# A streaming encoder's mixer: the third convolution input moved ahead of the query latents' split, the fourth into the attention stage, the output weights tied to the fifth head

## The chip, the cores and the metric

The kernel runs on one core of a Trainium2 chip. The metric is the device time of one execution in microseconds (us), as a median over runs. Engines are named as in the profile: PE is TensorE (matrix products; PEld its weight loads), DVE is VectorE, ACT is ScalarE, POOL is GpSimd, SP is SyncE, which here only issues DMAs. L145 means line 145 of the kernel.

## The reference, cut to what matters

Two layers of a Conformer-like block on 512 tokens of width 1024, all in float32:

```python
for l in range(2):
    x = x + 0.5 * swiglu(rms_norm(x), w_gate, w_up, w_down)      # FFN 1, inner width 2816
    h = rms_norm(x);  p = h @ w_in                               # the mixer's one input projection
    attn = mla_group(p[:384], p[384:640], p[640:672], ...)       # query latent, key/value latent, rotary key
    conv = conv_group(p[672:], ...)                              # GLU, causal depthwise conv k=31, LayerNorm, swish
    x = x + concat([attn, conv]) @ w_out
    x = x + 0.5 * swiglu(rms_norm(x), ...)                       # FFN 2
    x = rms_norm(x)
```

`mla_group` makes 8 heads of queries and keys from the latents (96 wide, RMS-normed, 32 of them rotated), chunk-causal scores, a softmax, and values of width 64. `conv_group` gates 512 channels and convolves each with its own 31 taps.

## The kernel before

**Layout and precision.** Features lie on partitions in tiles of 128, tokens along the free axis (512). Every float32 weight or activation that meets a matmul is split into a high part (an ACT cast to the matmul type, L134 or L150-157) and a low part (the rest, a DVE subtraction, L140 or L152-158), and `mm3` (L144) issues three matmuls for each product: high x high, high x low, low x high. These are the lines L145, L146 and L147.

**Loading.** `load_w` (L129) asks SP for a 128x1024 weight tile in a `raw` buffer (3 of them), lets ACT cast it to `wh` (4 buffers) and DVE subtract it to `wl` (4 buffers). With kind "sum", used for the first four output weight tiles, ACT writes the negated high part instead (L137) and a DMA issued by POOL (L138) adds the weights onto it in memory.

**The mixer of one layer** (`mix_body`, L527). The list `SEQ` (L44) gives the order of the steps after the first convolution input (L696):

- `q0 R c1 q1 q2`: query latents 0 to 2 (`latent_q`), the spread of the row norm R, and the second convolution input c1;
- `qo`: the split of the three query latents (`latent_q_out`, L157/L158, and their squares L174/L177);
- `k kt tt`: the key/value latent, its transposes (L620), the small per-token terms;
- `uq uk`: queries and keys from the latents. For each of four token blocks of keys, ACT copies and squares, DVE reduces, POOL raises to the power -1/2 (`rsqrt`, L163, tile `sck`), and DVE scales the keys into `kn` (L690 and L692). The last of these `rsqrt` instructions is kept as `order["keys"]`;
- `c2 c3`: the third and fourth convolution inputs.

`conv_in(c)` (L542) is two groups of 8 products, so 48 matmuls of 512 columns into two PSUM banks; `glu` (L531) follows: two DVE products with R (L533, L537), a sigmoid on ACT (L535) and a DVE product (L539) that writes u[c]. Convolutions 0 and 3 ("D") run their 30 taps on DVE (L814) into a PSUM bank; 1 and 2 ("A") run them as an ACT product (L818) and a POOL addition (L822) for each tap.

**Attention.** A loop over steps (L797) runs five stages with lags, from `ORDER`: `turn` (transposes of queries and keys of a head on PE, L718 and L723, then ACT L720 and DVE L725), `scores` one step later (L741 and the mask L742; DVE maxima L743; ACT exponentials L747), `turn_p` three later (L762, copies L765), `values` four later (L775, L780, L782) and `turn_out` five later (L793). So `turn(1)` comes before `scores(0)` in the text.

**What sets the order.** The text gives each instruction its rank; a planner then fixes, for each engine, the order in which its queue issues, taking by rank what its own timing says is ready, with buffers of one pool tag handed out from a fixed number. On the chip each engine runs its queue in that order and waits at semaphores. `tc.issue_after(i)` ties the instructions of its block to `i`: those of the block that run on the same engine as `i` are queued behind `i`; those of other engines get no tie. Three such ties matter here: the output weights' block (L803) behind `order["keys"]`, a POOL instruction; the POOL additions of convolution 1 from tap shift 16 on and all of convolution 2 (L821), behind the same one; and the early output groups (L829) behind the last scores.

**After attention.** POOL adds the four convolution outputs (L836 to L838), a matmul with a matrix of 1/512 gives their mean (L840), DVE subtracts it (L846), squares are summed (L178, L183), POOL takes the power, L197/L201 spread it, DVE and ACT finish the LayerNorm and swish (L856, L858), and the output projection runs over the attention part (which needs only `at`) and then the convolution part. Two of its groups come after the mean's matmul in the text, a third after the sums, and a fourth after the spread.

Of the kernel before, what the change touches and what calls it, by code (L numbers as in the profile page):

```python
# [39 lines left out]
WIDE = 5  # L40
CONV = "DAAD"
PAUSE = 16
SEQ = "q0 R c1 q1 q2 qo k kt tt uq uk c2 c3"
POOLW = "wo"  # L44
QFOLD = 0
GLUP = 0
# [24 lines left out]
def encoder_kernel(ctx: ExitStack, tc: tile.TileContext, xT, consts, vecs, rgain, wgu1, wd1,  # L71
# [20 lines left out]
    def tmp(w=S, dt=FP):  # L92
        return tmps.tile([P, w], dt, tag="t", name=nm("t"))

    def bank():
        return psum.tile([P, S], FP, tag="ps", name=nm("ps"))
# [32 lines left out]
    def load_w(src, w, kind="", two=False):  # L129
        raw = wpool.tile([P, WC], FP, tag="raw", name=nm("raw"), bufs=3)  # L130
        to = raw[:, :w]
        nc.sync.dma_start(out=to.rearrange("p (m c) -> p m c", m=2) if two else to, in_=src)
        hi = wpool.tile([P, WC], FR, tag="wh", name=nm("wh"))
        A.copy(hi[:, :w], raw[:, :w])  # L134
        lo = wpool.tile([P, WC], FR, tag="wl", name=nm("wl"))
        if kind == "sum":
            A.activation(lo[:, :w], raw[:, :w], AF.Copy, scale=-1.0)  # L137
            G.dma_start(out=lo[:, :w], in_=src, accum_op=ALU.add)  # L138
            return hi, lo
        (G if kind in POOLW.split() else V).tensor_tensor(lo[:, :w], raw[:, :w], hi[:, :w].bitcast(FP),  # L140
                                                          ALU.subtract)
        return hi, lo
# [67 lines left out]
    def group(o, w, rhs, ks, n):  # L210

        for k in ks:
            c = slice(k * P, (k + 1) * P)
            mm3(o, w[0][:, c], w[1][:, c], rhs[k][0], rhs[k][1], k == 0, k == n - 1)
# [308 lines left out]
    def mix(l, gx, norm, done):  # L523
        with tc.tile_pool(name="k", bufs=4) as kpool:
            mix_body(kpool, l, gx, norm, done)

    def mix_body(kpool, l, gx, norm, done):  # L527
        u, order = [], {}
        ys = [None if kind == "D" else kpool.tile([P, S], FP, tag="y", name=nm("y"), bufs=2) for kind in CONV]

        def glu(pa, pg):  # L531
            tg = tmp()
            V.tensor_tensor(tg, pg, R, ALU.mult)  # L533
            sg = tmp()
            A.activation(sg, tg, AF.Sigmoid)  # L535
            ta = tmp()
            V.tensor_tensor(ta, pa, R, ALU.mult)  # L537
            uc = slot()
            (G if GLUP else V).tensor_tensor(uc, ta, sg, ALU.mult)  # L539
            u.append(uc)  # L540

        def conv_in(c):  # L542
            pp = []
            for j in range(2):
                ps = bank()
                group(ps, load_w(wcv[l, 2 * c + j], WC, f"c{c}"), gx, range(KD), KD)
                pp.append(ps)
            glu(*pp)
# [148 lines left out]
        rm = norm()  # L697
        for step in SEQ.split():
            if step == "R":
                R = norm()  # L700
# [12 lines left out]
        heads = [{} for _ in range(H)]  # L713
# [83 lines left out]
        for step in range(H + 6):  # L797
            for stage, lag in STAGES:
                if 0 <= step - lag < H:
                    stage(step - lag)  # L800


        with tc.issue_after(order["keys"]):  # L803
            wo = [load_w(wout[l, m], WC, "sum") for m in range(WOP)]
        cw, cb = vv(l, "cw"), vv(l, "cb")
        for c in range(4):
# [4 lines left out]
            for k in range(CK - 2, -1, -1):  # L811
                s = CK - 1 - k
# [41 lines left out]
        for c in range(4):  # L854
            z = tmp()
            V.tensor_tensor(z, ys[c], pr, ALU.mult)  # L856
            s = tmp()
# [217 lines left out]
```

## Time and profile before

| | |
|---|---|
| median of 3 runs | 1817.16 us (1814.3 to 1822.64) |
| the profiled execution's own time | 1818.46 us |
| its span, first to last instruction | 1816.7 us, mean granted PE clock 0.993 |
| PE busy | 1761.6 us, 97% of the span |
| DVE, ACT, POOL busy | 1405.7, 949.7, 280.1 us |
| mixer of layer 1, about | 352 to 563 us |
| mixer of layer 2, about | 1250 to 1461 us |

A timeline row gives the start, the duration, the engine, the line, the operation, the tiles and, in brackets, how long the engine sat idle before it and what released it. Matmuls are pipelined: the start-to-start distance, not the shown duration, is what one costs. A row of the view of windows gives, for a stretch, its length and then for each engine its busy time and number of instructions; behind them stand the granted PE clock, the DMA share and GB/s.

### The profile page before, as it was taken

The page shows a single profiled execution, that of the slowest core. Times are in us where ns is not written, and L with a number is a line of the kernel's source. Part 1 is how long each engine was busy: PE and PEld are TensorE (multiplying, and loading weights), DVE is VectorE, ACT ScalarE, POOL GpSimd, SP SyncE. Part 2 cuts the span into 40 slices and gives each one's busy share as a digit, 9 for nine tenths or more (in the row PEclk, how much of TensorE's full clock was granted, in tenths as well). Part 3 has the DMA queues.
Part 4 walks back from the last instruction along what each step waited for, and adds up shares of the span by engine and source line. Part 5 has one row for each costly group of instructions (what it writes and reads, how often), then busy time and mean ns, then how long its engine had stood idle before and what let it go on. Part 6 is the DMA issues. An engine that isn't in the chain of part 4 may idle for free.

```text
span 1816.7 us, 22175 instructions
## 1 busy us (share of the span) xinstructions
PE 1761.6 (97%) x8160; PEld 1448.8 (80%) x8160; DVE 1405.7 (77%) x1983; ACT 949.7 (52%) x1471; POOL 280.1 (15%) x216
## 2 busy tenths in 40 slices
PE   8899999999899999999998999999999999999997
PEld 6688888888688778888876888888978787788885
DVE  8968887588958968878779678866989679678864
ACT  6444445457954634445544444444778445444442
POOL 4000000048932000000000000000688300000000
PEclk9999999999999999999999999999999999999998
DMA  8344434324124345343924445343250543444241
GB/s 287 122 156 152 149 105 139 117 87 127 37 115 117 125 154 163 113 142 107 286 70 131 136 129 162 105 128 118 74 151 1 161 118 119 159 139 153 91 151 58
DMA packets 119037, 234.09 MB, mean 129 GB/s; under 512 B 10256, under 2 KB 55696, under 8 KB 118928
## 3 DMA queue, kind: packets, MB, share of 16 engines
q1 hardware_dynamic: 115040, 219.72, 36.9%
q0 software_dynamic: 3456, 12.58, 3.9%
q8 instruction: 64, 1.05, 0.2%
q14 instruction: 45, 0.37, 0.1%
q10 hardware_dynamic: 432, 0.38, 0.1%
HBM read 207.47 MB, written 25.17 MB: 128 GB/s over the span
## 4 chain that ended last, share of the span: by engine, by line
PE 65%; issue 19%; DVE 5%; DMA 3%; ACT 3%; POOL 1%; SPq 1%; POOLq 0%; DVEq 0%; ACTq 0%
PE ps L145 20%; PE ps L147 20%; PE ps L146 20%; PE ps L775 2%; PE ps L741 1%; DVE wl L230 1%; DMA fr<-in_wgu 1%; ACT pr L818 1%; DMA r<-d 1%; PE ps L762 1%; DMA d<-e 1%; DVE fr L326 1%; ACT r L747 1%; POOL sck L163 0%; PE ps L201 0%
## 5 line engine op out<-in xcount | busy, mean ns | idle before, releaser
L145 PE MATMUL ps<-wh,r 128*128 128x512 f32 (+2 forms) x1392 | 520.3, 386 | 19.0 <-ACT wh L228 8.5
L147 PE MATMUL ps<-wh,r 128*128 128x512 f32 (+2 forms) x1392 | 530.8, 386 | 7.3 <-DVE r L158 7.1
L146 PE MATMUL ps<-wl,r 128*128 128x512 f32 (+2 forms) x1392 | 532.5, 384 | 0.0
L228 ACT CAST wh<-fr 128x1024 fp32r<-128x1024 f32 x256 | 267.9, 1049 | 239.2 <-PE ps L147 143.4
L147 PE MATMUL ps<-r,wl 128*128 128x512 f32 x1008 | 390.8, 390 | 0.5 <-POOL wl L140 0.5
L146 PE MATMUL ps<-r,wh 128*128 128x512 f32 x1008 | 391.1, 390 | 0.0
L145 PE MATMUL ps<-r,wh 128*128 128x512 f32 x1008 | 385.7, 393 | 3.2 <-ACT r L384 1.8
L230 DVE TENSOR_TENSOR wl<-fr,wh 128x1024 fp32r<-128x1024 f32 x256 | 312.6, 1224 | 76.2 <-ACT wh L228 75.2
L145 PEld LDWEIGHTS ps<-wh,r 128*128 128x128 f32 x1392 | 262.0, 189 | 73.8 <-ACT wh L228 10.3
L147 PEld LDWEIGHTS ps<-wh,r 128*128 128x128 f32 x1392 | 262.4, 189 | 62.5 <-DVE r L158 11.8
L146 PEld LDWEIGHTS ps<-wl,r 128*128 128x128 f32 x1392 | 262.4, 188 | 50.6 <-DVE wl L230 0.5
L134 ACT CAST wh<-raw 128x1024 fp32r<-128x1024 f32 (+2 forms) x150 | 148.8, 996 | 239.3 <-PE ps L146 89.2
L145 PEld LDWEIGHTS ps<-r,wh 128*128 128x128 f32 x1008 | 188.7, 188 | 48.3 <-ACT r L384 4.7
L146 PEld LDWEIGHTS ps<-r,wh 128*128 128x128 f32 x1008 | 189.2, 188 | 42.1 <-DVE r L385 1.8
L147 PEld LDWEIGHTS ps<-r,wl 128*128 128x128 f32 x1008 | 189.2, 188 | 40.8 <-POOL wl L140 1.3
L140 DVE TENSOR_TENSOR wl<-raw,wh 128x1024 fp32r<-128x1024 f32 (+3 forms) x134 | 157.6, 1177 | 76.4 <-ACT wh L134 75.6
L163 POOL TENSOR_TENSOR rtok<-vtok,minus_half 128x4 f32<-128x4 f32 x9 | 12.0, 1329 | 1089.4 <-DVE vtok L189 1089.4
L822 POOL TENSOR_TENSOR y<-y,pr 128x509 f32<-128x509 f32 (+15 forms) x120 | 157.8, 1316 | 49.9 <-ACT pr L818 42.4
L326 DVE TENSOR_TENSOR fr<-fr,fr 128x1024 f32<-128x1024 f32 x112 | 136.7, 1222 | 7.4 <-DMA fr<-in_wgu 7.2
L467 DVE TENSOR_TENSOR x<-ps,x 128x512 f32<-128x512 f32 x128 | 86.5, 686 | 44.1 <-PE ps L147 43.7
L385 DVE TENSOR_TENSOR r<-r,r 128x512 fp32r<-128x512 f32 x88 | 58.4, 682 | 70.7 <-ACT r L384 70.5
L356 ACT ACTIVATE e<-e,rtok 128x256 f32<-128x256 f32 x120 | 59.8, 507 | 71.6 <-DVE e L347 70.7
(164 smaller groups left out, 1724.1 us busy)
## 6 DMA issues: line engine op xcount, KB each, us to landing
fr<-in_wgu SPq DMA_DIRECT2D x176, 512.0 KB, 4.0
raw<-in_wd SPq DMA_DIRECT2D x64, 512.0 KB, 4.5
d<-e SPq DMA_DIRECT2D x176, 128.0 KB, 2.7
r<-d SPq DMA_DIRECT2D x88, 256.0 KB, 4.0
raw<-in_wd SPq DMA_DIRECT2D x32, 384.0 KB, 3.8
raw<-in_wcv SPq DMA_DIRECT2D x16, 512.0 KB, 3.3
raw<-in_wout SPq DMA_DIRECT2D x16, 512.0 KB, 3.7
raw<-in_wgu SPq DMA_DIRECT2D x8, 512.0 KB, 4.7
```

Of the source, the lines that this page charges most:

```text
L134: A.copy(hi[:, :w], raw[:, :w])
L140: (G if kind in POOLW.split() else V).tensor_tensor(lo[:, :w], raw[:, :w], hi[:, :w].bitcast(FP), ALU.subtract)
L145: T.matmul(o, lh, rh, start=first, stop=False, skip_group_check=free)
L146: T.matmul(o, lh, rl, start=False, stop=False, skip_group_check=free)
L147: T.matmul(o, ll, rh, start=False, stop=last, skip_group_check=free)
L228: A.copy(hi[:, :w], src[:, :w])
L230: V.tensor_tensor(lo[:, :w], src[:, :w], hi[:, :w].bitcast(FP), ALU.subtract)
L326: V.tensor_tensor(oh, ah, bh, ALU.add)
L356: A.activation(out[j][:, :h], src[j][:, :h], AF.Silu, scale=r)
L385: V.tensor_tensor(d, d.bitcast(FP), hi.bitcast(FP), ALU.subtract)
L467: V.tensor_tensor(xm, pd.rearrange("p (a t j) -> p t a j", a=4, t=NT), xm, ALU.add)
L822: order["conv"] = G.tensor_tensor(acc[:, s:], acc[:, s:], pr[:, s:], ALU.add).ins
```

## The change

The third convolution input moves from the end of the sequence to a place ahead of `qo`. The fourth leaves the sequence and is issued in the attention loop, in the step with number 1, right after the stage `turn`; so in the text it stands behind the transposes of heads 0 and 1 and ahead of `scores(0)`. The block that loads the first four output weight tiles is tied to the last instruction of `scores(4)`, a PE matmul, instead of to the last key `rsqrt`.

```diff
-SEQ = "q0 R c1 q1 q2 qo k kt tt uq uk c2 c3"
+SEQ = "q0 R c1 q1 q2 c2 qo k kt tt uq uk"
...
             for stage, lag in STAGES:
                 if 0 <= step - lag < H:
                     stage(step - lag)
+                if stage is turn and step == 1:
+                    conv_in(3)
...
-        with tc.issue_after(order["keys"]):
+        with tc.issue_after(heads[4]["s"]):
             wo = [load_w(wout[l, m], WC, "sum") for m in range(WOP)]
```

No instruction is added or removed by the text; only ranks and ties change. The POOL additions of the convolutions keep their tie to `order["keys"]`.

## Prediction

> **What bounds the kernel now.** The page first: TensorE is busy almost throughout, so only what moves its idle stretches, or its clock, can move the time.
>
> ```profile
> PE 1761.6 (97%) x8160; PEld 1448.8 (80%) x8160; DVE 1405.7 (77%) x1983; ACT 949.7 (52%) x1471; POOL 280.1 (15%) x216
> ```
>
> Then the view of windows over the first mixer. From its first product to the end of the four convolution inputs PE has no gap; around the start of attention it has one, and the granted clock falls with it.
>
> ```profile
> 352.00:452.00 100.00, 100.00 (x509) 87.02 (x508) 78.76 (x128) 61.98 (x112) 58.69 (x44) 1.00 0.33 98
> 450.00:460.00 10.00, 5.90 (x33) 4.52 (x32) 4.47 (x8) 9.98 (x16) 9.61 (x10) 0.95 0.80 181
> 460.00:470.00 10.00, 9.68 (x51) 6.32 (x50) 9.60 (x19) 9.99 (x24) 9.29 (x8) 0.88 0.20 42
> ```
>
> The timeline of PE shows the gap: the transposes of heads 0 and 1, then 4.10 us until the first scores.
>
> ```profile
> 452.01 0.60 PE L718 MATMUL ps<-cst,q 128*96 128x128 f32 x4
> 452.45 0.60 PE L723 MATMUL ps<-cst,kn 128*96 128x128 f32 x4
> 452.89 0.60 PE L718 MATMUL ps<-cst,q 128*96 128x128 f32 x4
> 453.32 0.60 PE L723 MATMUL ps<-cst,kn 128*96 128x128 f32 x4
> 458.02 0.49 PE L741 MATMUL ps<-r,r 96*128 96x128 f32 x2 [4.10 <-ACT r L720]
> ```
>
> ACT's timeline says why L720 came so late: output weight casts and convolution taps, then the fourth input's sigmoid, stand ahead of it.
>
> ```profile
> 453.12 1.03 ACT L134 CAST wh<-raw 128x1024 fp32r<-128x1024 f32 x1
> 454.05 1.05 ACT L137 ACTIVATE wl<-raw 128x1024 fp32r<-128x1024 f32 x1
> 455.01 0.69 ACT L818 ACTIVATE pr<-r,vec 128x487 f32<-128x487 f32 x1
> 455.60 0.61 ACT L535 ACTIVATE t<-t 128x512 f32<-128x512 f32 x1
> 456.12 1.27 ACT L818 ACTIVATE pr<-r,vec 128x486 f32<-128x486 f32 x2
> 457.30 1.24 ACT L720 ACTIVATE r<-ps,gqs 96x512 f32<-96x512 f32 x2
> ```
>
> What the gap is worth: 4.1 us idle, and in the two windows a clock short by 0.05 and 0.12 of 10 us each, 1.7 us more; 5.8 us a layer, 11.6 in both at most. The change aims there: 48 matmuls between the transposes and the first scores.
>
> [...]
>
> **A second bound, on POOL.** Most additions of convolutions 1 and 2 are queued behind the last key `rsqrt`. From there POOL works without a break until the convolution outputs are added.
>
> ```profile
> 438.75 2.75 POOL L163 TENSOR_TENSOR sck<-ssk,minus_half 128x8 f32<-128x8 f32 x1 [0.99 <-DVE scp L689]
> 441.46 0.92 POOL L138 DMA_DIRECT2D wl<-in_wout  x1
> ...
> 508.04 1.27 POOL L838 TENSOR_TENSOR t<-t,r 128x512 f32<-128x512 f32 x1
> ```
> ```profile
> L822 POOL TENSOR_TENSOR y<-y,pr 128x496 f32<-128x496 f32 (+29 forms) x45 | 57.4, 1276 | 4.2 <-ACT pr L818 1.2
> L138 POOL DMA_DIRECT2D wl<-in_wout x4 | 3.5, 880 | 0.0
> ```
>
> So the run from 441.5 to 509.3 is 67.8 us, of which 45 additions of 1.276 us are 57.4. Its result feeds the mean's matmul:
>
> ```profile
> 515.71 0.65 PE L793 MATMUL ps<-cst,t 128*128 128x128 f32 x4 [0.79 <-DVE t L782]
> 516.20 1.02 PE L840 MATMUL ps<-t,onesm 128*128 128x512 f32 x2
> ```
> ```profile
> 530.15 0.50 PE L145 MATMUL ps<-r,wh 128*128 128x512 f32 x1 [0.17 <-ACT r L151]
> ```
>
> The mean's matmul starts at 516.2 behind the last attention transposes: POOL has 6.9 us to spare. From there to the first product that needs the convolution (530.15) is a chain of 13.95 us, with the early output groups as PE's cover.
>
> **The change, step by step: the third input.** One matmul costs (452.01 - 430.25)/96 = 0.227 us, from the first matmul of the third input to the first transpose behind the fourth.
>
> ```profile
> 430.25 0.39 PE L145 MATMUL ps<-r,wh 128*128 128x512 f32 x1
> ```
>
> So 48 are 10.9 us, and everything from the latents to the keys comes 10.9 us later: the keys' last product at 441.1 instead of 430.25. PE had no gap where the input now goes, so nothing is won there. It brings two casts and two splits (1.03 on ACT, 1.22 on DVE each) and the `glu`; DVE has 21 us free in the 100, which hide them; uncovered they would cost some 5. The query latents' split now stands behind this `glu`. That order binds: in the trace the split starts right behind the sigmoid of the second input, though the first latent's products had ended by 369.66, when the spread follows them on PE.
>
> ```profile
> 369.66 1.02 PE L201 MATMUL ps<-t,ones 128*128 128x512 f32 x2
> ```
> ```profile
> 382.43 0.63 ACT L535 ACTIVATE t<-t 128x512 f32<-128x512 f32 x1
> 382.97 0.67 ACT L157 ACTIVATE r<-ps,vec 128x512 fp32r<-128x512 f32 x1
> ```
>
> I read this as buffers of one tag being handed out in the order of the text. The split's cover is then the key latent's matmuls; I take 0 for it, and up to 2 us if the squares come late.
>
> **The POOL run.** The last `rsqrt` moves with the keys, 10.9 us, less what leaves its path. DVE's rows show two splits of the fourth input's weights in that path; in the changed order they come earlier, in the place that the third's had.
>
> ```profile
> 435.05 1.22 DVE L140 TENSOR_TENSOR wl<-raw,wh 128x1024 fp32r<-128x1024 f32 x1
> 436.19 0.23 DVE L685 TENSOR_SCALAR ssk<-ssk,ckc 128x8 f32<-128x8 f32 x1
> 436.32 0.42 DVE L692 TENSOR_TENSOR kn<-ck,scp 128x256 f32<-128x256 f32 x1
> ...
> 444.24 1.48 DVE L692 TENSOR_TENSOR kn<-ck,scp 128x256 f32<-128x256 f32 x1
> ```
>
> Two times 1.22 is 2.4, so it ends at 441.5 + 10.9 - 2.4 = 450.0, and POOL's run at 517.8: 1.6 us behind today's 516.2. The second layer:
>
> ```profile
> 1333.51 4.22 POOL L163 TENSOR_TENSOR sck<-ssk,minus_half 128x8 f32<-128x8 f32 x2 [1.01 <-DVE ssk L685]
> 1337.68 0.91 POOL L138 DMA_DIRECT2D wl<-in_wout  x1
> ...
> 1404.02 1.26 POOL L838 TENSOR_TENSOR t<-t,r 128x512 f32<-128x512 f32 x1
> ```
> ```profile
> 1413.40 1.02 PE L840 MATMUL ps<-t,onesm 128*128 128x512 f32 x2
> ```
>
> `rsqrt` ends at 1337.7, POOL at 1405.3, the mean starts at 1413.4: 8.1 to spare. Here I take only one split off (its `rsqrt` wait is shorter): 10.9 - 1.2 - 8.1 = 1.6 us late. Bounds of the shift per layer: all of 10.9 (4.0 and 2.8 late), or 6 us, when neither is late.
>
> **The fourth input.** It should fill the 4.1 us. But the keys' last step ends at 445.7, 15.5 us after their last product; today two inputs (21.8 us) lie over that, afterwards one at most. If PSUM banks too are handed out in the order of the text, the input cannot start before the last bank of `turn(1)` is taken, thus before the first block of keys is ready. That is at 436.74, 6.5 us behind the keys' end; less the split at 435.05 it is 5.3. PE would fill 0.9 of it with the query transposes (two times 0.44) and idle 4.4. Then come 48 matmuls and the key transposes, and first scores at 441.1 + 5.3 + 10.9 + 0.9 = 458.2, against 458.02. The gap is moved, not closed; clock loss likewise. If banks go by readiness, the gap is 0 to 4 us; if every key block were needed, see below. In all but the last case attention ends before POOL's 517.8.
>
> **The output weights.** The block holds SP, ACT and POOL instructions and no PE one, so a tie to a PE matmul ties nothing; what goes is POOL's tie. Loads, casts and the POOL issues then come when buffers fall free, which is at the keys' end and during the fourth input, about as late as now. I take 0. It could gain up to 2.4 us a layer (four issues at some 0.6 us leave the POOL run), or cost 2.1 (POOL waits for one L134 and L137 ahead of the last `rsqrt`).
>
> **The sum.** 1.6 + 1.6 = 3.2 us on the profiled 1818.46, thus 1821.7. That execution lies 1.3 above the median of 1817.16, so the median becomes 1820.4; I say 1820.5, +0.2%. Half a per cent is 9.1 us, about what a measurement here can tell from no change (the three runs spread over 8.3 us); the edges are 1808.1 and 1826.2.
>
> **Rivals.** *The gap closes (faster).* The planner starts the fourth input at once, the transposes fall into it, and a less crowded DVE shortens the path from the keys to the last `rsqrt`. Then 5.8 us a layer come back (the second layer taken like the first): 1817.2 - 11.6 = 1805.6. For it: that path is 11.2 us today (441.5 - 430.25), and only part of it is the keys' own work. Against it: for the whole gain POOL must be done by 516.2 - 5.8 = 510.4, so its run must begin by 442.6, only 1.5 us after the keys' last product. Half of it, without passing the bound, is in my forecast. Chance 0.12.
>
> *PE waits for the whole of the keys (slower).* The place is PE's queue: transposes of all four key blocks ahead of the fourth input. PE then stands from 441.1 until the last block, 15.5 - 2.4 = 13.1 us, and first scores come at 441.1 + 13.1 + 10.9 + 0.9 = 466.0, 8.0 late, in both layers: 1817.2 + 16 = 1833. It decides as soon as the last blocks' transposes stand ahead of more than some 5 us of the input. Against it: the transposes depend on the keys block by block. Chance 0.16.
>
> *The tie does hold (slower).* If the weights really come in the fifth head, 4 x 2.1 = 8.4 us of ACT land where ACT is as full as in the quoted window (9.99 of 10). Taps give way and POOL's run stretches; if half is absorbed, 4.2 a layer: 1825.6. Chance 0.05.
>
> **How the numbers follow.** Forecast 0.67, rivals 0.12, 0.16, 0.05. Range 1811 to 1830: it takes in POOL's bounds (0 to 6.8 in sum), the 2 us of the latents' split in both layers, half of the gap won, and most of the slower rival; about 0.1 lies outside on each side. Faster by over half a per cent 0.11 (the first rival nearly whole), slower 0.19 (the second, a part of the third and the forecast's tail), same 0.70.
>
> **What would show it.** In the changed profile: the last `sck` near 450, with L822 running unbroken to about 517; L840 then released by POOL, not by L793; PE's idle time between keys and fourth input instead of ahead of the first scores; output weight casts still near 445 to 458. L840 at or before 516 with no gap ahead of the scores would refute me on the fast side, first scores later than 462 on the other.

## The result and the profile after

| | before | after |
|---|---|---|
| median | 1817.38 us (1814.3 to 1822.64, 9 runs) | 1825.48 us (1824.33 to 1827.65, 9 runs) |
| ratio to before, 95% interval | | 1.0044 (1.0034 to 1.0055) |
| span of the profiled execution | 1816.7 us | 1823.7 us |

The change makes the kernel about 8.1 us slower. Below, lines of the changed kernel from L801 on count two higher: L820 are ScalarE's taps, L824 the POOL additions, L840 the last sum, L842 the mean's matmul.

First the span is cut at a row that both kernels have twice in each mixer: the square sums on PE (L183), once ending the norm ahead of the mixer and once behind the mean's matmul. The timeline of PE, before and then after (columns as in the prediction; the second and fourth row of each are the ones behind the mean):

```profile
363.27 0.95 PE L183 MATMUL ps<-ones,acc 128*128 128x1 f32 x8
522.55 0.95 PE L183 MATMUL ps<-ones,acc 128*128 128x1 f32 x8
1260.78 0.95 PE L183 MATMUL ps<-ones,acc 128*128 128x1 f32 x8
1419.75 0.95 PE L183 MATMUL ps<-ones,acc 128*128 128x1 f32 x8
```
```profile
361.41 0.95 PE L183 MATMUL ps<-ones,acc 128*128 128x1 f32 x8
523.64 0.95 PE L183 MATMUL ps<-ones,acc 128*128 128x1 f32 x8
1263.03 0.95 PE L183 MATMUL ps<-ones,acc 128*128 128x1 f32 x8
1426.74 0.95 PE L183 MATMUL ps<-ones,acc 128*128 128x1 f32 x8
```

From norm to square sums the mixer takes 159.28 and 158.97 us before, 162.23 and 163.71 after: +2.95 and +4.74. Up to the first norm after is 1.86 us quicker, between the mixers 1.16 slower, and behind the last of these rows equal (396.95 and 396.96). The sum is the 7.0 us between the spans. PE's instructions outside the mixers stand in the same order in both kernels, so those -1.86 and +1.16 are what one execution differs from another; the loss is in the mixers. (These are single executions; the medians are 8.1 us apart.) This distance, from norm to square sums, is the measure of every run below.

Inside it, counted from the mixer's norm (layer 1 / layer 2):

| start of | before | after |
|---|---|---|
| first scores (L741) | 94.75 / 94.57 | 92.72 / 92.67 |
| last attention transposes (L793) | 152.44 / 152.13 | 151.23 / 151.51 |
| mean's matmul (L840, after L842) | 152.93 / 152.62 | 154.37 / 154.60 |
| square sums (L183) | 159.28 / 158.97 | 162.23 / 163.71 |

So attention begins 2 us earlier and ends 0.6 to 1.2 earlier; then everything is lost behind it, in two steps. PE's timeline of after at that place:

```profile
512.64 0.66 PE L793 MATMUL ps<-cst,t 128*128 128x128 f32 x4 [0.78 <-DVE t L782]
515.78 2.07 PE L842 MATMUL ps<-t,onesm 128*128 128x512 f32 x2 [2.49 <-POOL t L840]
516.87 1.42 PE L145 MATMUL ps<-r,wh 128*128 128x512 f32 x1
518.08 0.63 PE L146 MATMUL ps<-r,wh 128*128 128x512 f32 x1
...
1417.63 2.07 PE L842 MATMUL ps<-t,onesm 128*128 128x512 f32 x2 [2.44 <-POOL t L840]
1418.71 1.42 PE L145 MATMUL ps<-r,wh 128*128 128x512 f32 x1
1419.93 0.63 PE L146 MATMUL ps<-r,wh 128*128 128x512 f32 x1
...
1422.91 0.57 PE L147 MATMUL ps<-r,wl 128*128 128x512 f32 x1
1423.32 0.40 PE L145 MATMUL ps<-r,wh 128*128 128x512 f32 x1
```

Read it as follows. The mean's matmul waits 2.49 and 2.44 us for POOL's last sum; before, it followed L793 by 0.49 with no wait. Then it takes 2.07 us where it took 1.02, and the output matmuls behind it start 0.43 us apart at first (1419.93 to 1422.91 holds eight of them, seven distances of 0.426) and 0.23 apart later. From the mean's matmul to the square sums before needed 6.35 us in both layers (516.20 to 522.55, 1413.40 to 1419.75); after needs 7.86 and 9.11. The view of windows has the granted clock in the third column from the right; its rows for after:

```profile
460.00:470.00 10.00, 9.21 (x49) 6.27 (x48) 8.24 (x16) 10.00 (x30) 6.31 (x6) 0.83 0.20 39
...
510.00:520.00 10.00, 6.73 (x31) 4.88 (x31) 4.18 (x7) 3.75 (x7) 5.49 (x5) 0.83 0.00 0
...
1420.00:1430.00 10.00, 10.00 (x43) 8.19 (x42) 5.05 (x9) 2.42 (x4) 1.04 (x1) 0.84 0.00 0
```

Before had 1.00 in 510 to 520 and in 1420 to 1430. Why POOL is late shows in its timeline of after: the last key `rsqrt` ends at 446.08, 84.67 behind the norm (before 441.50, 78.23), and the additions behind it run with breaks until 515.73. Five of the breaks are waits for ACT's taps, 4.35 us in all; in before there were three, 1.18 us in all. The longest stands where ACT has its table load (1.28 us from 457.83) and the first exponentials between two taps (the taps at 457.13 and 461.27).

```profile
443.97 2.11 POOL L163 TENSOR_TENSOR sck<-ssk,minus_half 128x8 f32<-128x8 f32 x1
...
462.11 1.22 POOL L824 TENSOR_TENSOR y<-y,pr 128x487 f32<-128x487 f32 x1 [1.48 <-ACT pr L820]
464.31 1.21 POOL L824 TENSOR_TENSOR y<-y,pr 128x486 f32<-128x486 f32 x1 [0.98 <-ACT pr L820]
466.59 3.80 POOL L824 TENSOR_TENSOR y<-y,pr 128x485 f32<-128x485 f32 x3 [1.07 <-ACT pr L820]
...
514.47 1.26 POOL L840 TENSOR_TENSOR t<-t,r 128x512 f32<-128x512 f32 x1
```

And the start of attention, where the fourth input was to fill a gap of 4.10 us. PE's timeline of after:

```profile
440.28 0.60 PE L718 MATMUL ps<-cst,q 128*96 128x128 f32 x4
441.83 0.29 PE L723 MATMUL ps<-cst,kn 128*96 128x128 f32 x1 [0.95 <-DVE kn L692]
...
442.42 0.48 PE L145 MATMUL ps<-r,wh 128*128 128x512 f32 x1
...
454.13 0.38 PE L741 MATMUL ps<-r,r 96*128 96x128 f32 x2
...
459.64 0.70 PE L741 MATMUL ps<-r,r 96*128 96x256 f32 x2 [1.46 <-ACT r L747]
```

The gap is gone: 0.95 us for the first block of keys, and the fourth input starts at 442.42 behind that one block. A smaller wait of 1.46 comes at the second head's scores, whose bank the late exponentials still hold.

### The profile page after: what moved, and what is told of

The parts are those of the page before. It is cut to its first block, busy times and chain, and to the rows that moved or that the text cites. A ratio compares the mean times of both kernels' runs of the same rounds, so it can differ in the third digit from the quotient of the medians.

```text
span 1823.7 us, 22178 instructions
## 1 busy us (share of the span) xinstructions
PE 1767.5 (97%) x8160; PEld 1452.3 (80%) x8160; DVE 1403.6 (77%) x1983; ACT 953.4 (52%) x1471; POOL 273.6 (15%) x216
## 4 chain that ended last, share of the span: by engine, by line
PE 67%; issue 19%; DVE 4%; POOL 4%; ACT 3%; DMA 3%; SPq 0%; POOLq 0%; DVEq 0%; ACTq 0%
PE ps L145 21%; PE ps L147 20%; PE ps L146 20%; POOL y L824 2%; PE ps L741 2%; PE ps L775 1%; DVE wl L230 1%; DMA fr<-in_wgu 1%; DMA r<-d 1%; DMA raw<-in_wd 1%; PE ps L762 1%; PE ps L183 1%; ACT wh L228 0%; ACT pr L820 0%; PE ps L723 0%
## 5 line engine op out<-in xcount | busy, mean ns | idle before, releaser
L824 POOL TENSOR_TENSOR y<-y,pr 128x511 f32<-128x511 f32 (+14 forms) x120 | 158.4, 1320 | 59.7 <-ACT pr L820 51.8
L385 DVE TENSOR_TENSOR r<-r,r 128x512 fp32r<-128x512 f32 x88 | 58.3, 680 | 67.7 <-ACT r L384 67.6
L356 ACT ACTIVATE e<-e,rtok 128x256 f32<-128x256 f32 x120 | 59.7, 507 | 69.9 <-DVE e L347 69.3
```

The costliest lines, as they stand in the source:

```text
L356: A.activation(out[j][:, :h], src[j][:, :h], AF.Silu, scale=r)
L385: V.tensor_tensor(d, d.bitcast(FP), hi.bitcast(FP), ALU.subtract)
L824: order["conv"] = G.tensor_tensor(acc[:, s:], acc[:, s:], pr[:, s:], ALU.add).ins
```

## The experiments

Three theories were put to the test. *Keys theory:* the third input's move makes the keys late, POOL's tied additions end behind attention, PE waits and loses clock. *Place theory:* the fourth input among the turns delays exponentials and taps, and that starves POOL. *Tie theory:* the loosened tie of the output weights costs it. All runs are in one table; the span from norm to square sums is from each run's profile, and the ratios are to the kernel before on the same chip. Where a kernel has added or fewer lines, the mean's matmul is L840, L842, L843 or L844.

| run | median us | before, same chip | ratio, 95% interval | norm to square sums, layer 1 / 2 (before 159.28 / 158.97) |
|---|---|---|---|---|
| third only | 1824.81 | 1817.73 | 1.0036 (1.0023 to 1.0050) | 161.97 / 163.31 |
| fourth only | 1812.33 | 1817.73 | 0.9967 (0.9954 to 0.9980) | 157.22 / 155.79 |
| tie only | 1817.84 | 1817.73 | 1.0001 (0.9992 to 1.0009) | 159.22 / 159.63 |
| after, eight more free additions | 1836.24 | 1817.73 | 1.0102 (1.0088 to 1.0116) | 165.32 / 170.79 |
| after, four additions less | 1818.25 | 1816.63 | 1.0005 (0.9993 to 1.0017) | 158.15 / 158.37 |
| before, four additions more | 1816.82 | 1816.63 | 0.9999 (0.9989 to 1.0008) | 159.24 / 159.30 |
| before, eight additions more | 1823.84 | 1816.63 | 1.0036 (1.0024 to 1.0048) | 161.68 / 163.93 |
| after, a group ahead of the mean | 1822.43 | 1816.63 | 1.0031 (1.0020 to 1.0043) | 162.90 / 160.39 |
| after, third input put back | 1811.85 | 1818.15 | 0.9964 (0.9953 to 0.9976) | 155.27 / 158.99 |
| fourth behind the first turns | 1815.66 | 1818.15 | 0.9984 (0.9974 to 0.9994) | 159.30 / 156.69 |

**The three parts alone.** The third input alone:

```diff
-SEQ = "q0 R c1 q1 q2 qo k kt tt uq uk c2 c3"
+SEQ = "q0 R c1 q1 q2 c2 qo k kt tt uq uk c3"
```

> Three theories of the 8.1 us. Keys theory: the third input ahead of the split puts the keys 10.9 us later, GpSimd's 45 tied additions end behind attention, and TensorE's wait for them lowers its clock over the 24 output matmuls ahead of the square sums. Place theory: the fourth input among the turns makes exponentials and ScalarE's taps late, which starves GpSimd (4.35 us of waits in its run). Tie theory: the loosened tie of the output weights costs it. Here the third input alone is moved; the fourth stays ahead of the turns, the tie stays at the keys. Keys theory: the gap ahead of the first scores and the additions' end both stay, so at least the 1.4 + 2.0 us of waits and 1.5 + 2.8 us of slow matmuls: 6 to 11 us slower than before (1823 to 1828), the mean's matmul released by GpSimd. Place theory and tie theory: within 2 us of before.

Measured: 7.1 us slower, nearly the whole loss. PE's timeline of this run at the mean's matmul, layer 1 and layer 2:

```profile
518.06 1.12 PE L840 MATMUL ps<-t,onesm 128*128 128x512 f32 x2 [0.96 <-POOL t L838]
...
1416.37 1.17 PE L840 MATMUL ps<-t,onesm 128*128 128x512 f32 x2 [1.00 <-POOL t L838]
...
1417.76 0.63 PE L146 MATMUL ps<-r,wh 128*128 128x512 f32 x1
```

POOL is the releaser, as the keys theory has it; the other two had no change here. The waits are shorter than after's, since attention itself ends later. The slow matmuls follow in layer 2 (8.04 us to the square sums) but hardly in layer 1 (6.45), with nearly the same wait.

The late keys are only a part of POOL's delay, though. The last `rsqrt` ends 83.53 and 83.56 us behind the norm, 5.3 and 6.6 later than before, which is less than POOL's slack of 6.9 and 8.1. The rest comes from POOL's run itself: it takes 71.9 and 71.7 us instead of 67.8 and 67.6, with more waits for ACT's taps. Neither part alone uses up the slack; together they put POOL's end 9.4 and 10.7 later. POOL's timeline of this run:

```profile
462.46 1.22 POOL L822 TENSOR_TENSOR y<-y,pr 128x488 f32<-128x488 f32 x1 [1.46 <-ACT pr L818]
465.20 5.08 POOL L822 TENSOR_TENSOR y<-y,pr 128x487 f32<-128x487 f32 x4 [1.51 <-ACT pr L818]
```

The fourth input alone:

```diff
-SEQ = "q0 R c1 q1 q2 qo k kt tt uq uk c2 c3"
+SEQ = "q0 R c1 q1 q2 qo k kt tt uq uk c2"
...
+                if stage is turn and step == 1:
+                    conv_in(3)
```

> The fourth input alone stands between the second turns and the first scores; third input and tie as before. Keys theory: the keys come when they came in before, so GpSimd ends ahead of attention; the gap ahead of the first scores (4.1 us and about 1.7 us of lost clock in each layer) closes at least by the 2.0 us that after gained per layer: 4 to 8 us faster than before (1809 to 1813). Place theory: 4 us or more slower than before, the mean's matmul released by GpSimd. Tie theory: within 2 us of before or faster.

Measured: 5.4 us faster, and POOL is done ahead of attention (its last sum ends at 511.87, the mean's matmul starts at 513.48 with no wait). The place theory falls as an account of the loss. Its mechanism is there all the same: with the keys where they were (the last `rsqrt` ends 78.24 behind the norm, before 78.23), POOL's run takes 71.1 and 70.9 us instead of 67.8 and 67.6, again with waits for taps. It still ends 1.6 and 1.7 us ahead of the mean's matmul, so here it costs nothing. POOL's timeline:

```profile
464.25 1.21 POOL L824 TENSOR_TENSOR y<-y,pr 128x483 f32<-128x483 f32 x1 [1.64 <-ACT pr L820]
```

PE's timeline shows two smaller waits in place of the 4.10:

```profile
445.04 0.42 PE L723 MATMUL ps<-cst,kn 128*96 128x128 f32 x2 [1.27 <-DVE kn L692]
...
460.73 0.70 PE L741 MATMUL ps<-r,r 96*128 96x256 f32 x2 [2.04 <-ACT r L747]
```

The tie alone:

```diff
-        with tc.issue_after(order["keys"]):
+        with tc.issue_after(heads[4]["s"]):
             wo = [load_w(wout[l, m], WC, "sum") for m in range(WOP)]
```

> Only the output weights' tie is moved from the last key to the fifth head's last score matmul. Keys theory and place theory: within 1.5 us of before (1815.9 to 1818.9), and ScalarE's casts of these weights still stand ahead of the fifth head. Tie theory: 4 us or more slower.

Measured: no difference. ACT's timeline of this run has the last of the casts before even the first head's scores start (456.60), far ahead of the fifth head's:

```profile
448.02 1.03 ACT L134 CAST wh<-raw 128x1024 fp32r<-128x1024 f32 x1
...
453.24 1.04 ACT L137 ACTIVATE wl<-raw 128x1024 fp32r<-128x1024 f32 x1
```

The parts do not add up: +7.1 and -5.4 would make +1.7, after has +8.1. With the third input moved, the square sums come at nearly the same time with the fourth input in its new place (162.23 / 163.71) or not (161.97 / 163.31). With it attention ends 2.7 and 2.1 us earlier, but POOL sets the end: the mean's matmul starts only 1.15 and 0.67 earlier, and the clock takes that back (1.41 and 1.07 us more from there to the square sums). That the two come out so equal is in part chance.

**POOL's dose.** Does POOL's end alone make the loss? First it is taken away from after, then put into before:

```diff
 # after, four additions less
+                if c == 2 and s > CK - 5:
+                    continue
                 with tc.issue_after(order["keys"]) if s >= PAUSE or c > 1 else nullcontext():
...
 # before, 4 or 8 additions more, behind convolution 2's taps
+            if c == 2:
+                for _ in range(8):
+                    G.tensor_tensor(pr[:, s:], pr[:, s:], pr[:, s:], ALU.add)
```

> The changed kernel without the last four of the 30 additions of convolution 2 on GpSimd (their four taps are left out of the sum; ScalarE still makes the four products, so its queue is the same). Keys theory: GpSimd ends 4 x 1.27 = 5.1 us earlier, ahead of attention; the mean's matmul follows the last transposes by 0.49 us as before, and the 24 output matmuls run at 0.227 us. Then the square sums come 4.2 us earlier in layer 1 (162.23 to about 158.1 after the mixer's norm) and 5.4 in layer 2 (163.71 to 158.35): about 9.5 us faster than after, 1814 to 1818, at or below before. Place theory (late exponentials and taps hold attention itself) and tie theory: within 2 us of after, 1823.5 to 1827.5.

> The kernel before with four more additions (a scratch tile to itself, about 1.2 us each) on GpSimd behind convolution 2's, in each layer. Their 4.9 us fit into the 6.9 and 8.1 us that lie between GpSimd's last sum and the mean's matmul. Keys theory: no wait at the mean's matmul, within 1.5 us of before (1816 to 1819.5). A theory in which GpSimd's work slows its neighbours wherever it lies: 2 us or more slower.

> The kernel before with eight such additions in each layer: 9.8 us against 6.9 and 8.1 us of slack, all convolution inputs and keys where they were. Keys theory: the mean's matmul waits for GpSimd 2.9 us in layer 1 and 1.7 us in layer 2; with the slow matmuls that such a wait brought in after (1.5 to 2.8 us in each layer) 6 to 10 us slower than before (1824 to 1828). If only the wait counts and no clock: 4.5 us slower (1822). Place theory: within 2 us of before, since nothing was moved.

Measured: after without four additions is 1.0005 of before, 7 us below after, and its square sums stand at 158.15 and 158.37, where 158.1 and 158.35 were expected. (It leaves four taps out of the sum, so it answers a question and is no candidate. Its time, 1818.25, is just above the expected 1814 to 1818, though the mixers are 1.7 us shorter than before's; the rest lies outside the mixers.) PE's timeline of that run: no wait, no slow matmul, 6.35 us to the square sums.

```profile
513.94 0.66 PE L793 MATMUL ps<-cst,t 128*128 128x128 f32 x4 [0.78 <-DVE t L782]
514.43 1.02 PE L844 MATMUL ps<-t,onesm 128*128 128x512 f32 x2
...
520.78 0.95 PE L183 MATMUL ps<-ones,acc 128*128 128x1 f32 x8
```

Four additions more in before cost nothing; eight cost 7.2 us, with no input, key or tie moved. PE's timeline of the run with eight:

```profile
516.83 1.64 PE L843 MATMUL ps<-t,onesm 128*128 128x512 f32 x2 [1.21 <-POOL t L841]
...
518.69 0.63 PE L146 MATMUL ps<-r,wh 128*128 128x512 f32 x1
...
1416.96 2.07 PE L843 MATMUL ps<-t,onesm 128*128 128x512 f32 x2 [3.85 <-POOL t L841]
...
1425.71 0.95 PE L183 MATMUL ps<-ones,acc 128*128 128x1 f32 x8
```

Here the mean's matmul is 0.71 us later than before in layer 1 (153.64 against 152.93 behind the norm) and 2.56 in layer 2, where 2.9 and 1.7 were expected (the eight took 8.46 us in layer 1, not 9.8); but the square sums come 2.40 and 4.96 later. The rest, 1.69 and 2.40, is the part of slow matmuls (0.43 us apart from 518.69 on in layer 1), about as large as in after (1.51 and 2.76). So the same loss, of the same two terms, comes from POOL's end alone.

**Moving POOL's work ahead of the keys.** POOL has idle time before the keys, and `PAUSE` sets how many additions of convolution 1 may run there:

```diff
-PAUSE = 16
+PAUSE = 24
```

> The changed kernel, in which eight more of convolution 1's additions are free of the tie to the keys: 8 x 1.276 = 10.2 us of GpSimd's work move into its idle time ahead of the keys. Keys theory: GpSimd ends before attention does, the mean's matmul waits for TensorE's own order, and the 7.7 us of waits and slow matmuls (1.44 + 1.98 + 1.5 + 2.8) go: 1814 to 1819. If only the waits go and the clock stays low for another reason: about 1822. Place theory and tie theory: within 2 us of after (1823.5 to 1827.5). Counted against it: additions beside the keys slow VectorE's work on them, 1 to 2 us.

Measured: 18.5 us slower than before, against every expectation. The end did what the keys theory said: the mean's matmul follows the last transposes by 0.49 us, and the square sums follow it by 6.35. But in layer 1 attention began 7.6 us later than in after (first scores 100.33 behind the norm against 92.72); in layer 2 it began 9.9 later (102.58 against 92.67), which is not taken apart here. PE's timeline of the run shows the places up to the first key transposes:

```profile
416.58 0.44 PE L620 MATMUL ps<-cst,ck 128*128 128x128 f32 x2 [1.66 <-ACT ck L585]
419.55 1.61 PE L183 MATMUL ps<-ones,acc 128*128 128x1 f32 x8 [2.53 <-POOL acc L178]
450.20 0.28 PE L723 MATMUL ps<-cst,kn 128*96 128x128 f32 x1 [1.71 <-DVE kn L692]
```
```profile
420.00:430.00 10.00, 10.00 (x45) 9.88 (x46) 7.41 (x17) 6.64 (x20) 6.83 (x10) 0.67 0.18 61
```

The freed additions and their taps now stand in POOL's and ACT's queues in front of the latents' square sums (L178 on POOL) and copies (L585 on ACT). PE waits 1.66 and 2.53 us, of which after had 0.63, then the clock is at 0.67 for a window (3.3 us), and 0.76 more goes at the key transposes: 1.66 + 1.90 + 3.3 + 0.76 = 7.6. The theory of the end stood; its remedy overlooked that both queues are in use ahead of the keys. Beside an addition DVE's scaling of a block of keys (L692) took 1.48 us in the profile of before (at 444.24), against 0.42 beside a `rsqrt` (at 436.32). How much an addition alone costs there, without its tap, was not tried.

**Work in place of the wait.** One output group goes ahead of the mean's matmul:

```diff
-E1 = 0
+E1 = 1
```

> The changed kernel with one of the two output groups (12 matmuls, 2.7 us) placed ahead of the mean's matmul in place of behind it, so that TensorE works through the 2.5 us in which it waited for GpSimd. Keys theory with its clock part: the wait and the slow matmuls go, less what VectorE still needs behind the mean: 3 to 6 us faster than after (1819.5 to 1822.5). If the clock does not fall because of the wait: the 24 matmuls stay at 0.427 us and the gain is at most the 2 us of the two short waits. Place and tie theory: within 2 us of after.

Measured: 1.0031 of before, 2.4 us below after by the ratios and 3.1 by the medians, at the edge of what was expected; the intervals of the two ratios overlap, so the size is not sure. In layer 1 the mean's matmul takes 1.02 us, no matmul from there to the square sums is slow, and the square sums wait for DVE in its place:

```profile
519.73 1.02 PE L842 MATMUL ps<-t,onesm 128*128 128x512 f32 x2
...
525.61 1.02 PE L183 MATMUL ps<-ones,acc 128*128 128x1 f32 x8 [2.11 <-DVE acc L178]
```

(The profiled execution was itself 5.7 us longer than the run's median; the clock had fallen to 0.63 in its window from 460 to 470, so its 162.90 in layer 1 may not be typical.) The expectations for this run and for the four additions less spoke of 24 slow matmuls; the rows of after show that only the first of them are, two or three in layer 1 and nine in layer 2.

**Only the third input put back,** the other two parts as in after:

```diff
-SEQ = "q0 R c1 q1 q2 c2 qo k kt tt uq uk"
+SEQ = "q0 R c1 q1 q2 qo k kt tt uq uk c2"
```

> The changed kernel with only its first part undone: the third convolution input stands behind the keys again, the fourth stays between the second turns and the first scores and the tie at the fifth head. Keys theory, with the tie worth nothing: as the fourth input alone, 4 to 7 us faster than before (1810 to 1813.5), so 12 to 15 us faster than after. If parts of the 8.1 us need the tie and the fourth input together: 1815 or more.

Measured: 6.3 us faster than before, 0.9964, the same as the fourth input alone (0.9967) within the intervals. It beats both kernels, and the third input is what stood against it.

**The fourth input one place earlier:**

```diff
-                if stage is turn and step == 1:
+                if stage is turn and step == 0:
```

> The fourth input alone, one place earlier: behind the first head's turns in place of the second's. In the run with the fourth input alone TensorE still waits 2.04 us at the second head's scores, because ScalarE has the sigmoid of that input and a table load ahead of the first exponentials. If that order is the reason, the sigmoid comes some 1.3 us earlier (the second turns' eight transposes now stand behind it) and the wait shrinks by about that: 0 to 3 us faster than the fourth input alone (1809 to 1812.5). If a new wait of the second turns on their bank or of the first scores takes its place: 2 us or more slower than that run.

Measured: 0.9984 of before, where the fourth input alone had 0.9967. The medians put it some 3 us above that run, but the two intervals overlap (0.9974 to 0.9994, 0.9954 to 0.9980), so that it is slower is not sure; the gain that was hoped for is not there. The wait for exponentials at the second head's scores is gone in layer 1 and 0.21 us in layer 2, and another stands in its place: 2.71 us in layer 1 and 1.56 in layer 2, for the second head's keys (DVE, L725). Attention takes 61.2 and 59.2 us from first scores to last transposes, where the fourth input alone had 58.4 in both. That is a new wait of the kind that the expectation named as its rival, at another place than the two it named.

## Why the prediction was right and where it was wrong

The sign and the range held (1825.48 in 1811 to 1830); the size did not: +8.1 us against +3.2.

**Right: POOL becomes the bound, but the size by luck.** The sum rested on the mean's matmul waiting for POOL and coming 1.6 us late in each layer. It came 1.44 and 1.98 late, released by L840, not by L793. The sizes inside were off and cancelled:

- The last `rsqrt` came 6.4 and 7.7 us later behind the norm, not 8.5 and 9.7. In layer 1 the keys' last product came 11.9 later, not 10.9, but from there to the end of the last `rsqrt` it took 5.8 us, where the prediction left 11.2 - 2.4 = 8.8. The two weight splits did leave that path; besides, DVE's first reduction of the keys (L681) starts 3.7 us ahead of their last product, where it started 0.9 ahead before. Which of these made the rest is not shown.
- 6.4 and 7.7 are less than the slack of 6.9 and 8.1. The mean's matmul comes later than before only because POOL's run grew as well, to 69.6 and 69.9 us from 67.8 and 67.6. "From there POOL works without a break" was a misreading: the row shown for L822 has 4.2 us of idle time, 1.2 of it behind ACT, and this wait for taps is what grew, to 4.35 us in layer 1. The forecast had no term for it.

**Wrong: "from there to the first product that needs the convolution (530.15) is a chain of 13.95 us", taken as unchanged.** It grew by 1.5 us in layer 1 and 2.8 in layer 2 (the first such product stands at 531.24 and 1434.35 in after, so 15.46 and 16.72). All of this lies between the mean's matmul and the square sums (7.86 - 6.35 = 1.51, 9.11 - 6.35 = 2.76): PE's cover for the chain stands in PE's own queue ahead of the square sums, so when it runs at half clock (granted 0.50 from 515.33 to 518.74 and from 1416.45 to 1423.27) it is the chain. The prediction counted clock loss for the gap ahead of the scores and none for the wait that it forecast itself; that term, put at nothing, measured 4.27 us in sum, more than the 3.2 of the wait. 3.42 us of later start (1.44 + 1.98) and 4.27 us of slow matmuls make the mixers' whole 7.7 us.

**Wrong, without effect on the sum: "the gap is moved, not closed".** The prediction let the first block of keys come 5.3 us behind the keys' last product and PE idle 4.4. It came 1.55 behind (440.28 to 441.83) and PE idled 0.95, with DVE's work on the keys begun 3.7 us ahead of that product; the fourth input then began behind that single block, as forecast. Attention so ended 0.6 to 1.2 us earlier, and POOL took it back. In the run without the third input's move the same step was worth the 5.4 us.

**Right: the tie is worth nothing** (1.0001; one of the four POOL issues, L138, now stands ahead of the last `rsqrt` instead of behind it), and nothing was won by the third input's move: at L183 PE even waits 0.63 us for POOL in the new order.

Of the rivals, the closing gap described what PE did at the start of attention, and its own objection, that POOL must be done in time, is what kept it from paying. The two slower rivals did not occur: first scores came 2 us earlier, and the last output weight cast (L137, 455.06) still comes at the start of attention, long before the fifth head.

## What to carry to other kernels

When a wait is forecast on the busiest engine, price also what stands behind it in that engine's queue at a lower clock; here that was more than the wait itself in sum (4.27 us against 3.42). Before moving work ahead of the instruction that a queue's remaining work is tied behind, compare that queue's slack (6.9 and 8.1 us here) with the shift, and with what its run gains in breaks (up to 4.1 us here) when its suppliers are busy with the next stage: past it, every gain elsewhere in the stage is spent waiting. Parts of a change that meet at one bound do not add up, so measure each alone: one was worth -5.4 us and was hidden by another's +7.1.

## What the runs showed of the hardware

**Behind short waits PE ran slow, and not each time.** After waits of 2.49 and 2.44 us in after, 1.00 in the run with the third input alone, 1.21 and 3.85 in before with eight additions (all with 0.78 or 0.79 us idle just before), matmuls started some 0.43 us apart instead of 0.23 for some 3 to 6 us. After 0.96 in the run with the third input alone they hardly did: its granted clock is 1.00 from 510 to 520, where that wait lies, and 0.87 from 1410 to 1420, where the wait of 1.00 lies. Within one execution of the kernel with the third input put back, the second head's scores wait 1.85 us in layer 1 and 2.04 in layer 2 for the same reason:

```profile
459.01 0.70 PE L741 MATMUL ps<-r,r 96*128 96x256 f32 x2 [1.85 <-ACT r L747]
...
1350.69 0.70 PE L741 MATMUL ps<-r,r 96*128 96x256 f32 x2 [2.04 <-ACT r L747]
```

In layer 1 the clock stays at 1.00 (453 to 473), in layer 2 it is 0.50 for 10.24 us; attention then takes 61.6 us in layer 2 instead of 57.9, and that layer's gain is gone (158.99 against 155.27).

**How busy PE was around these waits.** The traces hold the granted clock with the times of its changes; in before and after it is 1.00 or 0.50, and the shortest stretch at 0.50 is 3.41 us. In windows of that length the two waits look like this (the view of windows, the clock third from the right):

```profile
457.96:461.37 3.41, 2.36 (x14) 1.62 (x15) 3.15 (x6) 3.40 (x10) 3.11 (x3) 1.00 1.01 237
461.37:464.78 3.41, 2.99 (x16) 1.55 (x13) 3.41 (x8) 3.41 (x12) 1.85 (x2) 1.00 0.13 25
...
1348.90:1352.31 3.41, 1.62 (x7) 0.91 (x8) 1.26 (x3) 3.40 (x8) 3.33 (x4) 1.00 0.75 177
1352.31:1355.72 3.41, 3.05 (x14) 2.35 (x13) 2.29 (x4) 3.41 (x11) 1.74 (x2) 0.50 0.64 126
```

In layer 1 PE is busy for 2.36 of the 3.41 us in which the wait ends, and the clock stays at 1.00. In layer 2 nearly the whole wait lies in the first window, PE is busy for 1.62 of its 3.41 us, and the clock is 0.50 in the second. In after PE was busy for 0.66 and 1.37 of the 3.41 us ahead of the two falls at the mean's matmul (511.92 to 515.33 and 1413.04 to 1416.45). No run changed how a wait lies and nothing else, so what decides whether a wait costs clock is not shown.
